# Attention core of a hybrid decoder trunk: head pairs in 64-row score tiles and 64-column value tiles, mask and row maximum in one vector operation

**Chip, cores, metric.** One Trainium2 chip, all eight cores, each with one batch element of 4096 rows. The metric is device time of the slowest core in microseconds (us).

## The reference, cut to what matters

```python
# per layer: x += 1/2 FFN ; x += mixer ; x += 1/2 FFN   (each between two RMS norms)
# layer 0: RG-LRU mixer, layer 1: sliding-window attention, 16 query heads, 2 key/value heads, head size 64
kk = jnp.concatenate([k_prev, k], axis=2)            # 128 previous + 128 current keys
scores = jnp.einsum('bnqkgd,bnskd->bnkgqs', q, kk) * scale
diff = qi + ATTN_BLOCK - kj
band = (diff >= 0) & (diff < WINDOW)                 # 128 keys, the current one included
scores = jnp.where(valid, scores, NEG_INF)
probs = softmax(concatenate([scores, sink], -1))[..., :-1]
out = jnp.einsum('bnkgqs,bnskd->bnqkgd', probs, vv)
```

## The kernel before

The program is a list of operations in eight tiles of 512 rows. Two tiles are under way at a time ("chains"). A list scheduler in Python, with a duration for every operation, settles the fixed order of each engine and which of the eight PSUM banks an operation gets. A chain may hold six banks. The scheduler asks for one bank at a time:

```python
for h in o.ps:                       # the PSUM banks that operation o uses
    if h.bank is None:
        if not self.free or self.held.get(h.chain, 0) >= self.limit:
            return None
        x = min(f[0] for f in self.free) + (PE_HOP if o.eng == "pe" else HOP)
        if x > r:
            r = x
```

At the start of an attention stage the query buffer `QZ` is cleared, since each of the two heads of a pair gets a full 128-row operand whose other half is zero:

```python
dve(s, lambda e: e.memset(QZ[64:128, :, 0, :], 0.0), [], rQZ, n=4096)
dve(s, lambda e: e.memset(QZ[0:64, :, 1, :], 0.0), [], rQZ, n=4096)
```

The stage then has 16 steps of four heads. Step i, shortened:

```python
hh2 = [Ps(s), Ps(s)]                                     # two PSUM banks
for hp in range(2):
    items = []
    for hf in range(2):                                  # score, then mask added by a matmul with IDENT
        items += group(hh2[hp], [QZ[:, c, hf, n*128:(n+1)*128], IDENT[:, :]],
                       [KT[:, n*128:n*128+256], mk[:, :]], lo=hf*256, hi=hf*256+256)
    mm(s, [hh2[hp]], items, ...)                         # one TensorE group for each bank
for hp in range(2):
    dve(... tensor_reduce(out=max, in_=PS[h.bank], op=max))           # row maximum
    dve(... tensor_scalar(out=neg, in0=max, scalar1=-SCALE, scalar2=NSMAX, op0=mult, op1=min))
    # two exponentials of 128x256 on ScalarE, read from PSUM, with their sums; the sinks' exponential
# phaseB: divide (VectorE); phaseB2: 8 transposes on TensorE, copied out by ScalarE
# phaseC: value product, 8 matmuls of 128 columns with zero-padded values, copied out by ScalarE
```

Phases B, B2 and C run one, two and four steps later. TensorE matmuls of the other chain's FFN are meant to fill the time in which ScalarE and VectorE do the softmax.

## Time and profile before

| | before |
|---|---|
| fast runs | 4862.4, 4862.7 us |
| all runs, median | 4899.4 us |
| profiled run | 4863.6 us, fast, granted clock 0.991 to 0.993 |
| TensorE busy | 4663.1 us of 4863.6 |

In the slow state one die has a lower granted clock (0.83 in such a run here). (The median of 4936 us in the prediction is one of the four runs; the median of the four is 4899.)

### The profile page before, as it was taken

How to read it: one execution, taken by the hardware profiler on the slowest of the kernel's cores; microseconds unless marked ns; L12 is line 12 of the kernel's file. 1: busy time of each engine (PE TensorE's matmuls, PEld its weight loads, DVE VectorE, ACT ScalarE, POOL GpSimd, SP SyncE). 2: the span in 40 equal slices, each digit the busy share in tenths (PEclk: the TensorE clock that was granted, in tenths of full speed). 3: DMA queues.
4: the chain of work that ended last, by engine and by line, in shares of the span. 5: the costliest groups of instructions: out<-in, count | busy, mean ns of one | idle time of the engine just before them, and what ended most of it. 6: DMA issues, size and time to landing. Idle time of an engine off the chain costs nothing.

```text
span 4863.6 us, 76832 instructions; the slowest of 8 cores (4837.4 to 4863.6 us)
## 1 busy us (share of the span) xinstructions
PE 4663.1 (96%) x24640; PEld 2246.3 (46%) x24640; DVE 2007.6 (41%) x3580; ACT 2239.4 (46%) x4396; POOL 813.7 (17%) x1365
## 2 busy tenths in 40 slices
PE   6999999898999999999999999999999999999998
PEld 3444445453444444445444444454544444445453
DVE  2355326462235442546223553264622455236441
ACT  2556327372246732647225573273721656227451
POOL 2231321311212021121110201012111012011011
PEclk9999999999999999999999999999999999999999
DMA  9999998979988867483875655536456455543445
GB/s 195 186 191 180 203 179 185 191 167 218 208 202 200 186 194 179 125 202 121 240 190 169 174 158 173 161 104 208 140 179 182 161 166 162 161 158 120 142 150 137
DMA packets 238423, 844.59 MB, mean 174 GB/s; under 512 B 26448, under 2 KB 26704, under 8 KB 238032
## 3 DMA queue, kind: packets, MB, share of 16 engines
q1 hardware_dynamic: 171648, 615.77, 38.4%
q0 software_dynamic: 66384, 223.90, 29.1%
q8 instruction: 209, 3.42, 0.3%
q14 instruction: 182, 1.49, 0.1%
HBM read 932.89 MB, written 113.77 MB: 215 GB/s over the span
## 4 chain that ended last, share of the span: by engine, by line
PE 80%; DMA 7%; ACT 4%; issue 4%; DVE 3%; POOL 2%; SPq 0%; DVEq 0%; POOLq 0%; ACTq 0%
PE psall L333 78%; DMA W<-wgu 2%; DMA W<-wdn 2%; PE psall L427 2%; ACT XN L800 1%; DVE XT L415 1%; DMA X<-x 1%; DMA W<-wmix 1%; POOL NS L406 1%; DMA bdn<-W 1%; PE psall L840 1%; DMA W<-bgu 0%; DMA out<-X 0%; POOL NS L404 0%; DMA W<-bdn 0%
## 5 line engine op out<-in xcount | busy, mean ns | idle before, releaser
L333 PE MATMUL psall<-XN,W 128*128 128x512 bf16 x12864 | 2840.4, 380 | 23.5 <-DMA W<-wgu 13.8
L333 PEld LDWEIGHTS psall<-XN,W 128*128 128x128 bf16 x12864 | 1252.7, 98 | 1513.6 <-issue 56.4
L333 PE MATMUL psall<-W,BIG 128*128 128x512 bf16 x5632 | 1242.4, 380 | 27.2 <-DMA W<-wdn 20.7
L547 DVE TENSOR_TENSOR BIG<-SG,psall 128x512 bf16<-128x512 bf16 x704 | 477.1, 685 | 1149.0 <-PE psall L333 1059.8
L545 ACT ACTIVATE SG<-psall 128x512 bf16<-128x512 f32 x704 | 414.4, 595 | 1108.5 <-PE psall L333 1080.4
L333 PEld LDWEIGHTS psall<-W,BIG 128*128 128x128 bf16 x5632 | 549.1, 98 | 688.1 <-issue 45.9
L568 ACT ACTIVATE HY<-psall 128x512 bf16<-128x512 f32 x256 | 150.5, 595 | 808.8 <-PE psall L333 808.8
L573 DVE TENSOR_TENSOR FB<-psall,GR 128x512 f32<-128x512 f32 x240 | 157.5, 686 | 788.6 <-ACT HY L568 410.8
L404 POOL TENSOR_SCALAR NS<-NS 128x1 f32<-128x1 f32 x256 | 133.1, 520 | 1118.4 <-ACT BIG L515 806.9
L432 ACT ACTIVATE XN<-psall 128x1024 bf16<-128x1024 bf16 x192 | 196.3, 1022 | 264.5 <-PE psall L427 263.4
L406 POOL TENSOR_TENSOR NS<-NS,NHALF 128x1 f32<-128x1 f32 x384 | 305.5, 798 | 51.6 <-POOL NS L404 9.0
L415 DVE SCALAR_TENSOR_TENSOR XT<-X,NS,GI 128x1024 bf16<-128x1024 f32 x192 | 244.9, 1279 | 141.1 <-POOL NS L406 127.9
L800 ACT ACTIVATE XN<-psall,ST 128x256 bf16<-128x256 f32 x512 | 246.5, 509 | 1.5 <-DVE ST L820 0.9
L333 PE MATMUL psall<-W,HY 128*128 128x512 bf16 x1024 | 234.5, 379 | 10.9 <-ACT FB L846 3.9
L411 ACT ACTIVATE XT<-X 128x1024 bf16<-128x1024 f32 x192 | 202.3, 1056 | 54.7 <-DVE X L467 26.4
L972 POOL DMA_DIRECT2D W<-wgu x199 | 110.2, 555 | 693.1 <-PE psall L333 565.2
L791 DVE TENSOR_REDUCE ST<-psall 128x1 f32<-128x512 f32 x256 | 168.7, 683 | 137.2 <-PE psall L333 137.1
L467 DVE SCALAR_TENSOR_TENSOR X<-FB,NS,X 128x1024 f32<-128x1024 f32 x160 | 205.1, 1282 | 40.8 <-POOL NS L406 38.7
L972 POOL DMA_DIRECT2D W<-wdn x143 | 77.2, 540 | 739.4 <-PE psall L333 679.2
L427 PE MATMUL psall<-IDENT,XT 128*128 128x128 bf16 x1536 | 119.5, 224 | 80.0 <-DVE XT L415 67.6
L427 PEld LDWEIGHTS psall<-IDENT,XT 128*128 128x128 bf16 x1536 | 99.4, 100 | 135.6 <-issue 111.5
L333 PEld LDWEIGHTS psall<-W,HY 128*128 128x128 bf16 x1024 | 97.6, 98 | 129.4 <-issue 17.6
(95 smaller groups left out, 3166.3 us busy)
## 6 DMA issues: line engine op xcount, KB each, us to landing
W<-bgu SPq DMA_DIRECT2D x505, 512.0 KB, 4.0
W<-bdn SPq DMA_DIRECT2D x209, 512.0 KB, 3.7
W<-wgu POOLq DMA_DIRECT2D x199, 512.0 KB, 13.6
W<-wdn POOLq DMA_DIRECT2D x143, 512.0 KB, 12.5
W<-bmix SPq DMA_DIRECT2D x117, 512.0 KB, 4.1
bgu<-W SPq DMA_DIRECT2D x88, 512.0 KB, 9.5
W<-wmix POOLq DMA_DIRECT2D x51, 512.0 KB, 10.5
GI<-rows SPq DMA_DIRECT2D x48, 512.0 KB, 5.7
```

The lines of the kernel that those rows point to most:

```text
L333: ins = e.matmul(out() if callable(out) else out, lhsT=lhs() if callable(lhs) else lhs, rhs=rhs() if callable(rhs) else rhs, start=st, sto ...
L406: pool(s, lambda e: e.tensor_tensor(out=NS[s][:, o:o + 1], in0=NS[s][:, i:i + 1], in1=NHALF[:, :], op=ALU.pow), [("NS", s, i), "NHALF"], [ ...
L411: act(s, lambda e: e.activation(out=XT[s][:, b % 2, :], in_=X[s][:, b, :], func=AF.Square, scale=1.0 / 32, accum_out=NS[s][:, 16 + b:17 + b]),
L415: dve(s, lambda e: e.scalar_tensor_tensor(out=XT[s][:, b % 2, :], in0=X[s][:, b, :], scalar=NS[s][:, 20 + b:21 + b], in1=GI[s][:, :], op0= ...
L427: ins = e.transpose(PS[h.bank].bitcast(BF16)[:, c * 128:(c + 1) * 128], XT[s][:, b % 2, c * 128:(c + 1) * 128], IDENT[:, :])
L432: act(s, lambda e: e.activation(out=XN[s][:, :, b * 128:(b + 1) * 128], in_=PS[h.bank].bitcast(BF16).rearrange("p (c q) -> p c q", c=NCH), ...
L467: dve(s, lambda e: e.scalar_tensor_tensor(out=X[s][:, b, :].rearrange("p (h t) -> p h t", h=2), in0=FB[s][:, c:c + d + 1:d, :], scalar=R, ...
L545: act(s, lambda e, g=g, hg=hg: e.activation(out=SG[s][:, g, :], in_=PS[hg.bank], func=AF.Silu), [hg], [("SG", s, g)], tab="silu", ps=[hg])
L547: dve(s, lambda e, g=g, j=j, hu=hu: e.tensor_tensor(out=A[:, j, :], in0=SG[s][:, g, :], in1=PS[hu.bank], op=ALU.mult), [("SG", s, g), hu], ...
L791: dve(s, lambda e, h=h, mxc=mxc: e.tensor_reduce(out=ST[s][:, kk, mxc:mxc + 1], in_=PS[h.bank], axis=AX.X, op=ALU.max), [h], [("ST", s, kk ...
L800: act(s, lambda e, h=h, hf=hf, hh=hh, ngc=ngc: e.activation(out=EEs[kk][:, hh, :], in_=PS[h.bank][:, hf * 256:(hf + 1) * 256], func=AF.Exp ...
L972: return e.dma_start(out=W[:, slot, 0:ncols], in_=ap[:, 0:ncols])
```

## The change

The intent: do the two heads of a pair at once in the upper and the lower 64 rows of the array, without zero padding; do the value product in two column halves at once; add the mask where the row maximum is taken, on VectorE. The core of the diff (layout, value copies with their two small memsets of 128x256, and checks at the end are cut):

```diff
+            need = sum(h.bank is None for h in o.ps)
+            if need:
+                if len(self.free) < need or self.held.get(o.chain, 0) + need > self.limit:
+                    return None
+                x = sorted(f[0] for f in self.free)[need - 1] + (PE_HOP if o.eng == "pe" else HOP)
...
-            dve(s, lambda e: e.memset(QZ[64:128, :, 0, :], 0.0), [], rQZ, n=4096)
-            dve(s, lambda e: e.memset(QZ[0:64, :, 1, :], 0.0), [], rQZ, n=4096)
...
+                for ci in range(2):
+                    for hf in range(2):
+                        items.append((bank(hh2[hf], ci * 256, ci * 256 + 256),
+                                      Q[hf * 64:hf * 64 + 64, 2 * g + ci, n * 128:(n + 1) * 128],
+                                      KT[hf * 64:hf * 64 + 64, n * 128:n * 128 + 256], True, True))
+                mm(s, hh2, items, rQ[2 * g] + rQ[2 * g + 1] + rKT, hh2, n=256)
+                G.ops[-1].occ = 2 * (256 / 2400.0 + 0.02)
...
+                    dve(s, lambda e, ...: e.tensor_tensor_reduce(
+                        out=SP[k2][:, hf, :, :], in0=PS[h.bank]..., in1=mk[:, :]..., scale=-SCALE,
+                        scalar=NSMAX[:, 0:1], op0=ALU.add, op1=ALU.min, accum_out=ST[s][:, kk, ngc:ngc + 1]), ...)
...                      # exponentials now read SP in SBUF
+                for k2 in range(2):
+                    for hf in range(2):
+                        items.append((lambda hf=hf: PS[h.bank][hf * 64:hf * 64 + 64, 0:256],
+                                      VP[:, n + k2, hf * 64:hf * 64 + 64], PT4[:, hf, k2, :, :], k2 == 0, k2 == 1))
```

Since a pair of tiles writes two banks, the two score groups of a step have become one TensorE group, and the scheduler now gives it both banks together or none.

More of the change, by code (lines that the diff above doesn't have):

```diff
@@ L158, in ready @@
         if self.banks:
-            for h in o.ps:
-                if h.bank is None:
-                    if not self.free or self.held.get(h.chain, 0) >= self.limit:
-                        return None
-                    x = min(f[0] for f in self.free) + (PE_HOP if o.eng == "pe" else HOP)
-                    if x > r:
-                        r = x
+            need = sum(h.bank is None for h in o.ps)
[3 more added lines that the diff above has]
+                x = sorted(f[0] for f in self.free)[need - 1] + (PE_HOP if o.eng == "pe" else HOP)
+                if x > r:
+                    r = x
         return r
@@ L287, in build_program @@
         KC = sb("KC", [128, 128], BF16)
-        VC = sb("VC", [128, 2, 128], BF16)
+        VC = sb("VC", [128, 128], BF16)
         NHALF = sb("NHALF", [128, 1], F32)
@@ L367, in build_program @@
         dve(P, lambda e: e.memset(KC[:, :], 0.0), [], ["KC"], n=128)
-        dve(P, lambda e: e.memset(VC[:, :, :], 0.0), [], ["VC"], n=256)
+        dve(P, lambda e: e.memset(VC[:, :], 0.0), [], ["VC"], n=128)
         dve(P, lambda e: e.tensor_scalar(out=NSINK[:, :], in0=BC[:, 128:144], scalar1=-1.0, scalar2=None,
@@ L708, in attn @@
             BIGb = BIG[s][:, :].bitcast(BF16)
-            QZ = BIGb[:, 0:8192].rearrange("p (c h t) -> p c h t", c=8, h=2)
-            KT = BIGb[:, 8192:8192 + 128 + T]
-            VP = BIGb[:, 8832:8832 + (NB_ + 1) * 256].rearrange("p (b h m) -> p b h m", b=NB_ + 1, h=2)
-            rQ = [bigu(s, c * 512, (c + 1) * 512) for c in range(8)]
-            rQZ = bigu(s, 0, 4096)
-            rKT = bigu(s, 4096, 4416)
-            rVP = bigu(s, 4416, 4416 + (NB_ + 1) * 128)
+            Q = BIGb[:, 0:4096].rearrange("p (c t) -> p c t", c=8)
+            KT = BIGb[:, 4096:4096 + 128 + T]
+            VP = BIGb[:, 4736:4736 + (NB_ + 1) * 128].rearrange("p (b m) -> p b m", b=NB_ + 1)
+            SP = [BIG[s][:, 2816 + kk * 1024:2816 + (kk + 1) * 1024].rearrange("p (f c q) -> p f c q", f=2, c=2)
+                  for kk in range(2)]
+            rQ = [bigu(s, c * 256, (c + 1) * 256) for c in range(8)]
+            rKT = bigu(s, 2048, 2368)
+            rVP = bigu(s, 2368, 2368 + (NB_ + 1) * 64)
+            rSP = [bigu(s, 2816 + kk * 1024, 2816 + (kk + 1) * 1024) for kk in range(2)]
             XNf = XN[s][:, :, :].rearrange("p c t -> p (c t)")
@@ L728, in attn @@
                 early_io(s, final)
-            dve(s, lambda e: e.memset(QZ[64:128, :, 0, :], 0.0), [], rQZ, n=4096)
-            dve(s, lambda e: e.memset(QZ[0:64, :, 1, :], 0.0), [], rQZ, n=4096)
-            dve(s, lambda e: e.memset(VP[:, 1:NB_ + 1, 0, 64:128], 0.0), [], rVP, n=256)
-            dve(s, lambda e: e.memset(VP[:, 1:NB_ + 1, 1, 0:64], 0.0), [], rVP, n=256)
             dve(s, lambda e: e.tensor_copy(out=KT[:, 0:128], in_=KC[:, :]), ["KC"], rKT, n=128)
-            dve(s, lambda e: e.tensor_copy(out=VP[:, 0, :, :], in_=VC[:, :, :]), ["VC"], rVP, n=256)
+            dve(s, lambda e: e.tensor_copy(out=VP[:, 0, :], in_=VC[:, :]), ["VC"], rVP, n=128)
             pc = Piece(("akv",))
@@ L750, in attn @@
             dve(s, lambda e: e.tensor_tensor(
-                out=VP[:, 1:NB_ + 1, 0, 0:64], in0=psv()[:, :, 0:64],
-                in1=BC[:, 0:64].unsqueeze(1).broadcast_to([128, NB_, 64]), op=ALU.add),
-                [hv, "BC"], rVP, n=256, ps=[hv])
-            dve(s, lambda e: e.tensor_tensor(
-                out=VP[:, 1:NB_ + 1, 1, 64:128], in0=psv()[:, :, 64:128],
-                in1=BC[:, 64:128].unsqueeze(1).broadcast_to([128, NB_, 64]), op=ALU.add),
-                [hv, "BC"], rVP, n=256, ps=[hv])
+                out=VP[:, 1:NB_ + 1, :], in0=psv(), in1=BC[:, 0:128].unsqueeze(1).broadcast_to([128, NB_, 128]),
+                op=ALU.add), [hv, "BC"], rVP, ps=[hv])
             dve(s, lambda e: e.tensor_copy(out=KC[:, :], in_=KT[:, T:T + 128]), rKT, ["KC"], n=128)
-            dve(s, lambda e: e.tensor_copy(out=VC[:, :, :], in_=VP[:, NB_, :, :]), rVP, ["VC"], n=256)
+            dve(s, lambda e: e.tensor_copy(out=VC[:, :], in_=VP[:, NB_, :]), rVP, ["VC"], n=128)
             for pq in range(4):
@@ L765, in attn @@
                     proj(s, pc, c2 * 1024, XN, "XN", h)
-                    for hf in range(2):
-                        act(s, lambda e, c=c, hf=hf, h=h: e.activation(
-                            out=QZ[hf * 64:hf * 64 + 64, c, hf, :], in_=PS[h.bank][hf * 64:hf * 64 + 64, :],
-                            func=AF.Identity, bias=PV[hf * 64:hf * 64 + 64, BQ + c:BQ + c + 1], scale=1.0),
-                            [h, "PV"], rQ[c], ptr=1, ps=[h])
+                    act(s, lambda e, c=c, h=h: e.activation(
+                        out=Q[:, c, :], in_=PS[h.bank], func=AF.Identity, bias=PV[:, BQ + c:BQ + c + 1], scale=1.0),
+                        [h, "PV"], rQ[c], ptr=1, ps=[h])
             steps = [(n, g) for n in range(NB_) for g in range(4)]
@@ L778, in phaseA @@
                 mk = MASK0 if (k == 0 and n == 0) else MASK
+                k2 = i % 2
                 hh2 = [Ps(s), Ps(s)]
-                for hp in range(2):
-                    c = 2 * g + hp
-                    items = []
+                items = []
+                for ci in range(2):
                     for hf in range(2):
-                        items += group(hh2[hp], [QZ[:, c, hf, n * 128:(n + 1) * 128], IDENT[:, :]],
-                                       [KT[:, n * 128:n * 128 + 256], mk[:, :]], lo=hf * 256, hi=hf * 256 + 256)
-                    mm(s, [hh2[hp]], items, rQ[c] + rKT + ["IDENT", "MASK", "MASK0"], [hh2[hp]], n=256)
@@ L787, in phaseA @@
-                for hp in range(2):
-                    h = hh2[hp]
-                    mxc = 0 if hp == 0 else 14
-                    ngc = 1 if hp == 0 else 15
-                    dve(s, lambda e, h=h, mxc=mxc: e.tensor_reduce(
-                        out=ST[s][:, kk, mxc:mxc + 1], in_=PS[h.bank], axis=AX.X, op=ALU.max),
-                        [h], [("ST", s, kk, 0, hp)], ps=[h])
-                    dve(s, lambda e, mxc=mxc, ngc=ngc: e.tensor_scalar(
-                        out=ST[s][:, kk, ngc:ngc + 1], in0=ST[s][:, kk, mxc:mxc + 1], scalar1=-SCALE,
-                        scalar2=NSMAX[:, 0:1], op0=ALU.mult, op1=ALU.min),
-                        [("ST", s, kk, 0, hp), "NSMAX"], [("ST", s, kk, 1, hp)], n=4, ptr=1)
-                    for hf in range(2):
-                        hh = 2 * hp + hf
-                        act(s, lambda e, h=h, hf=hf, hh=hh, ngc=ngc: e.activation(
-                            out=EEs[kk][:, hh, :], in_=PS[h.bank][:, hf * 256:(hf + 1) * 256],
-                            func=AF.Exp, bias=ST[s][:, kk, ngc:ngc + 1], scale=SCALE,
+                        items.append((bank(hh2[hf], ci * 256, ci * 256 + 256),
+                                      Q[hf * 64:hf * 64 + 64, 2 * g + ci, n * 128:(n + 1) * 128],
+                                      KT[hf * 64:hf * 64 + 64, n * 128:n * 128 + 256], True, True))
@@ new lines, in phaseA @@
+                mm(s, hh2, items, rQ[2 * g] + rQ[2 * g + 1] + rKT, hh2, n=256)
+                G.ops[-1].occ = 2 * (256 / 2400.0 + 0.02)
+                G.ops[-1].dur = G.ops[-1].occ + 0.17
+                for hf in range(2):
+                    h = hh2[hf]
+                    ngc = hf
+                    dve(s, lambda e, h=h, hf=hf, ngc=ngc: e.tensor_tensor_reduce(
+                        out=SP[k2][:, hf, :, :], in0=PS[h.bank].rearrange("p (c q) -> p c q", c=2),
+                        in1=mk[:, :].unsqueeze(1).broadcast_to([128, 2, 256]), scale=-SCALE, scalar=NSMAX[:, 0:1],
+                        op0=ALU.add, op1=ALU.min, accum_out=ST[s][:, kk, ngc:ngc + 1]),
+                        [h, "NSMAX", "MASK", "MASK0"], [("ST", s, kk, 1, hf), ("SP", s, k2, hf)]
+                        + (rSP[k2] if hf == 0 else []), ptr=1, ps=[h])
+                    for ci in range(2):
+                        hh = 2 * ci + hf
+                        act(s, lambda e, hf=hf, ci=ci, hh=hh, ngc=ngc: e.activation(
+                            out=EEs[kk][:, hh, :], in_=SP[k2][:, hf, ci, :],
+                            func=AF.Exp, bias=ST[s][:, kk, ngc:ngc + 1], scale=-1.0,
@@ L803, in phaseA @@
                             accum_out=ST[s][:, kk, 2 + hh:3 + hh]),
-                            [h, ("ST", s, kk, 1, hp)],
+                            [("ST", s, kk, 1, hf), ("SP", s, k2, hf)] + rSP[k2],
                             [("EE", s, kk, hh), ("ST", s, kk, 2, hh)] + ([rEE[kk]] if hh == 0 else [])
                             + (rXN if i == 0 and hh == 0 else []),
-                            n=256, ptr=1, tab="exp", ps=[h], acc=True)
-                    act(s, lambda e, hp=hp, ngc=ngc: e.activation(
-                        out=ST[s][:, kk, 6 + 2 * hp:8 + 2 * hp],
-                        in_=BC[:, 128 + 4 * g + 2 * hp:128 + 4 * g + 2 * hp + 2],
+                            n=256, ptr=1, tab="exp", ps_in=False, acc=True)
@@ L811, in phaseA @@
+                    act(s, lambda e, hf=hf, ngc=ngc: e.activation(
+                        out=ST[s][:, kk, 6:10].rearrange("p (c f) -> p f c", f=2)[:, hf, :],
+                        in_=BC[:, 128 + 4 * g:132 + 4 * g].rearrange("p (c f) -> p f c", f=2)[:, hf, :],
                         func=AF.Exp, bias=ST[s][:, kk, ngc:ngc + 1], scale=1.0),
-                        [("ST", s, kk, 1, hp), "BC"], [("ST", s, kk, 3, hp)], n=4, ps_in=False, ptr=1, tab="exp")
+                        [("ST", s, kk, 1, hf), "BC"], [("ST", s, kk, 3, hf)], n=4, ps_in=False, ptr=1, tab="exp")
@@ L853, in phaseC @@
                 items = []
-                for ci in range(2):
-                    items += group(h, [VP[:, n + k2, hf, :] for hf in range(2) for k2 in range(2)],
-                                   [PTs[kk][:, (ci * 2 + hf) * 2 + k2, :] for hf in range(2) for k2 in range(2)],
-                                   lo=ci * 128, hi=ci * 128 + 128)
-                mm(s, [h], items, rVP + rPT[kk] + rXN, [h], n=128)
+                PT4 = PTs[kk].rearrange("p (c f k) q -> p f k c q", c=2, f=2)
+                for k2 in range(2):
+                    for hf in range(2):
+                        items.append((lambda hf=hf: PS[h.bank][hf * 64:hf * 64 + 64, 0:256],
+                                      VP[:, n + k2, hf * 64:hf * 64 + 64], PT4[:, hf, k2, :, :], k2 == 0, k2 == 1))
+                mm(s, [h], items, rVP + rPT[kk] + rXN, [h], n=256)
+                G.ops[-1].occ = 2 * (256 / 2400.0 + 0.05)
+                G.ops[-1].dur = G.ops[-1].occ + 0.17
                 act(s, lambda e: e.activation(
@@ L896, in build_program @@
         emit(nc, G, eng, esem, wsem, vsem, bsem, W, (wgu, wdn, wmix), (bgu, bdn, bmix), limit, report)
+        for sem in bsem:
+            if sem.v:
+                nc.sync.wait_ge(sem.h, sem.v)
         for s in range(NS_):
@@ L901, in build_program @@
                         nc.sync.wait_ge(sem.h, sem.v)
+    mybir.codegen_inst_isa_subclasses(nc)
     return nc
```

## The prediction

> **What bounds the kernel now.** I read the page's engine table first, then the cores, the slices, the groups of instructions, the stretches of the attention core, and last the timeline there.
>
> ```profile
> PE 4663.1 (96%) x24640; PEld 2246.3 (46%) x24640; DVE 2007.6 (41%) x3580; ACT 2239.4 (46%) x4396; POOL 813.7 (17%) x1365
> PEclk9999999999999999999999999999999999999999
> DMA  9999998979988867483875655536456455543445
> PE 80%; DMA 7%; ACT 4%; issue 4%; DVE 3%; POOL 2%; SPq 0%; DVEq 0%; POOLq 0%; ACTq 0%
> ```
>
> TensorE is 96% busy over 4863.6 us, and 80% of the chain that ended last is TensorE; the other engines are below half. Since its ends are modelled, I checked with spacings. A run of 32 matmuls of 512 columns takes 7.07 us, which is 31 spacings and a last one of 0.38, so one spacing is 0.216 us. All 19776 matmuls of that width then fill 4270 us. The 1024 of 256 columns (0.110 us each, below) fill 113, and the 2560 transposes and 1280 other matmuls of 128 columns (0.056) fill 215. That is 4598 of 4864 us, and only some 265 us are gaps. So TensorE time removed should shorten the run almost one for one, unless something else then ends last. All cores are within 0.5% at a clock of 0.99, so this is the fast state; the listed median of 4936 is 1.5% above its fastest run, and I start from 4863.
>
> The attention core appears eight times (one per tile of 512 rows, 16 steps each, 128 steps in all):
>
> ```profile
> 4641.95 0.27 PE L333 MATMUL psall<-BIG 128*128 128x256 bf16 x1
> 4642.06 0.27 PE L333 MATMUL psall<-MASK,IDENT 128*128 128x256 bf16 x1
> ...
> 4642.72 0.27 PE L333 MATMUL psall<-MASK,IDENT 128*128 128x256 bf16 x1
> ...
> 4642.83 0.61 PE L840 MATMUL psall<-IDENT,XN 128*128 128x128 bf16 x8
> ...
> 4645.00 0.61 PE L333 MATMUL psall<-FB,BIG 128*128 128x128 bf16 x8
> ```
>
> The second column is the duration. Eight score and mask matmuls start 0.110 us apart (0.77 us over seven spacings). The eight transposes follow without a gap. The value product is eight matmuls in 0.61 us, of which the last is 0.22, so they are 0.056 us apart. Between these groups stand runs of 8 or 16 matmuls of the other tile's FFN: those are the filler that keeps TensorE busy while ScalarE and VectorE do the softmax.
>
> ```profile
> 790.00:850.00 60.00, 54.32 (x446) 34.05 (x444) 45.98 (x149) 55.45 (x172) 6.40 (x10) 1.00 0.70 170
> ...
> 4435.00:4490.00 55.00, 53.69 (x389) 30.99 (x388) 37.09 (x96) 44.00 (x117) 9.89 (x12) 1.00 0.36 112
> ```
>
> The columns after the length are busy us of PE, PEld, DVE, ACT and POOL, then the clock, the DMA share and GB/s. In the first attention stretch ScalarE is busy 92% of the time and the DMA engines 70%. In the later ones ScalarE is at 80%, TensorE at 98%, DMA at 36%.
>
> [...] The trace shows weight loads of 98 ns hidden behind 256 columns; whether 64-column loads stay hidden no run shows yet. [...] the reduction of 128x512 takes 683 ns, the product with a PSUM operand (L547) 685 ns. So I expect about 0.7 us for the joined operation.
>
> **The change part by part.**
>
> *Score and mask matmuls.* Before: 8 per step by 0.110 = 0.88 us. After: 4 score matmuls in 64-row tiles, alternating upper and lower rows, each pair at once: 2 pairs by 0.110 = 0.22 us. Saved: 0.66 us a step, by 128 = 84 us. Of this the mask alone is 0.44 us a step.
>
> *Value product.* Before: 8 by 0.056 = 0.446 us. After: 4 matmuls of 256 columns, in pairs for the two halves of the columns: 2 by 0.110 = 0.22 us. Saved: 0.226 us, by 128 = 29 us.
>
> *Together* 0.886 us a step, 113 us or 2.3% if tiling were free. [...] Each step goes from full array to row tiles and back, and to column tiles and back: four changes of mode, three where the two groups stand side by side. A full drain would show as the tail that a matmul has beyond its spacing, 0.27 - 0.11 = 0.16 us. Four of them are 0.64 us, which leaves 0.25 us a step (31 us). On the other side, the changed kernel's own schedule table allows 0.02 and 0.05 us above streaming for each pair, 0.14 us a step, which leaves 0.75 (95 us). Those look like fitted numbers, so I lean that way and take 0.25 us of overhead: 0.886 - 0.25 = 0.64 us a step, **81 us** off TensorE.
>
> *VectorE.* 256 reductions (683 ns) become 256 joined operations of about 0.7 us with a 128x512 float32 output; 256 small operations of 207 ns go (51 us busy), and the memsets of L729 to L732 (60 us busy). None of it is on the path, apart from 4.8 us that TensorE spends behind two of the memsets.
>
> *ScalarE.* The query eviction becomes 64 operations of 128x512 in place of 128 of 64x512, which take 682 ns each although they have half the rows: 44 us fewer. The exponentials read float32 from SBUF instead of PSUM. The comparable pair on the page is 689 ns (L656, PSUM) against 714 ns (L670, SBUF), so 512 by 25 ns = 13 us more. ScalarE's work in a step stays about what it is.
>
> *Buffers.* Score banks are freed by VectorE alone, before the exponentials. TensorE now waits 10.0 us for L808 and 8.2 us for L800, mostly for such banks; I credit 5 us. Against it, a step now takes two banks at once.
>
> *Where the saving falls.* Two of the eight attention stretches lie in the first quarter, where weights come in as float32 and DMA is 70% and 50% busy; TensorE waits 34.5 us in all for wgu and wdn. A quarter of 81 us is 20; I take half of that as lost to weights that come no sooner. At the end the last attention core has only the previous tile's last FFN beside it, and needs 16 by 0.64 = 10 us more filler: I take 3 us as lost. Sum: 81 + 5 - 10 - 3 = 73 us. **4863 - 73 = 4790 us**, 1.5% faster.
>
> **The rivals.**
>
> *Mode changes eat it.* If every change drains and the weight load must then follow (another 0.06 us or so, as between a late load and its matmul at the start of such a group), four changes cost 0.9 us, the whole saving, and the time stays at about 4860. [...] Against it: the kernel's own occupancy figures. I give it one in five.
>
> *ScalarE becomes the pace.* In the first attention stretch the evictions of the value product come 3.34 us apart, ScalarE being 92% busy:
>
> ```profile
> 799.78 0.43 ACT L859 ACTIVATE HY<-psall 128x256 bf16<-128x256 f32 x1
> 803.12 0.47 ACT L859 ACTIVATE HY<-psall 128x256 bf16<-128x256 f32 x1
> 806.46 0.51 ACT L859 ACTIVATE HY<-psall 128x256 bf16<-128x256 f32 x1
> ```
>
> Then a step takes what it took, and the TensorE time freed is idle unless more FFN work is put in. For it: that pace. Against it: a tile has four FFNs of 528 matmuls, 114 us each, and the core needs only 10 us more filler, so the freed time comes back as an FFN that ends sooner; and the later stretches have ScalarE at 80%. If it holds for half the stretches, the gain is some 35 us: 4830.
>
> *Free tiling and waits that go too.* If pairs cost nothing (113 us) and half the gaps that TensorE has in the attention core go with the mask matmuls, the gain is 120 to 140 us: 4725 to 4745. For it: about 30 us of waits for L808, L800, L846 and L823 stand there. Against it: those come from the softmax, which isn't shorter.
>
> **Range and chances.** The author's overhead with nothing lost gives 4768, mine 4790, ScalarE's pace 4830, full drains 4860, free tiling 4735. A new order of the whole static schedule adds some 15 us either way. So 4735 to 4860 holds it 8 times in 10. Two per cent is 97 us, 4766: that asks for the author's figure with no loss, or better. I give it 0.25, within 2% 0.72, slower 0.03.
>
> **What would show it.** In the changed kernel's profile: no MASK matmul; the second matmul of a pair starting a few ns after the first (right) or 0.11 us after (tiles not at once); a first matmul after a score or value group that follows within 0.05 us (no drain) or 0.16 us and more (drain); the joined VectorE operation at 0.68 to 0.75 us; exponentials some 25 ns longer; TensorE's busy share still 95% or more. It would be wrong if the share fell below 94% with ScalarE over 90% in all eight stretches, if the joined operation took over 1 us, or if waits for weights grew by more than 20 us.

## The result

| | before | after |
|---|---|---|
| fast runs | 4862.4, 4862.7 | 4721.1, 4721.3, 4724.1 |
| median of all | 4899.4 | 4722.7 |
| ratio of fast runs | | 0.9711 (0.9683 to 0.9739) |

Ratios are the mean time of one kernel's fast runs over that of the other's fast runs of the same rounds, so not quite the ratio of the medians. The gain is 141 us, 2.9%, where 73 us was forecast; 4722.7 lies 12 us below the stated range. The direction was right, the gain forecast was half of what came.

The same lines of the page as the prediction shows, of the kernel after:

```profile
PE 4563.4 (97%) x23616; PEld 2115.3 (45%) x23616; DVE 1929.0 (41%) x3540; ACT 2234.1 (47%) x4348; POOL 791.0 (17%) x1358
PEclk9999999999999999999999999999999999999999
DMA  9999999999988767664774654445466454443544
PE 82%; DMA 8%; issue 3%; DVE 2%; ACT 2%; POOL 2%; SPq 0%; POOLq 0%; DVEq 0%; ACTq 0%
```

TensorE still bounds it. But its busy time fell by 100 us and the span by 143, so over 40 us came from time in which TensorE did nothing. (The busy time counts the tail of a matmul, 380 ns recorded for 512 columns that start 216 ns apart, and a halved clock as busy, so the split by starts below finds more.) The groups of instructions that are new, one shape a line (busy us, mean ns of one, then idle time before):

```profile
L785 DVE CUSTOM_DVE_ANT_1 BIG<-psall,MASK,NSMAX 128x512 f32<-128x512 f32 x256 | 182.8, 747 | 206.6 <-PE psall L333 158.0 <-ACT XN L793 48.6
L793 ACT ACTIVATE XN<-BIG,ST 128x256 bf16<-128x256 f32 x512 | 253.4, 497 | 1.6 <-DVE ST L785 1.2
L333 PE MATMUL psall<-BIG 64*128 64x256 bf16 x512 | 47.4, 274 | 0.0
L333 PE MATMUL psall<-FB,BIG 128*64 128x256 bf16 x320 | 32.8, 283 | 1.0
```

The joined operation takes 747 ns (plus an accumulator read of 83 ns), as expected. The exponentials read SBUF at 497 ns; in the kernel before they took 509 from PSUM, so the loss expected there did not come. With everything else as in the changed kernel, they take 490 from PSUM (run in_psum below), so the source alone makes 7 ns here. And the timeline of TensorE in a core (start, duration):

```profile
3144.41 0.39 PE L333 MATMUL psall<-BIG 64*128 64x256 bf16 x4
3144.73 0.62 PE L833 MATMUL psall<-IDENT,XN 128*128 128x128 bf16 x8
3145.28 0.41 PE L333 MATMUL psall<-FB,BIG 128*64 128x256 bf16 x4
3145.62 0.39 PE L333 MATMUL psall<-BIG 64*128 64x256 bf16 x4
```

Four score matmuls take 0.32 us until the next group starts. Eight transposes, which fill 0.45 us, are followed by the value tiles after 0.55. The starts in the trace say why: the second of a pair starts 3 to 4 ns after the first, the second pair 116 ns (row tiles) or 130 ns (column tiles) after that, and wherever the mode changes the next start is 93 to 97 ns later than the streaming asks (311 ns after a 512-column matmul in place of 216, 149 after a transpose in place of 56, 201 and 205 after the last tile in place of about 108). So pairs do run at once, and **a change of mode costs 0.095 us**, 440 times: 42 us. What fills the 95 ns the trace doesn't separate. Within one mode the next weight load starts some 214 ns ahead of its matmul of 512 columns; after a change, unless TensorE also waited there, the first load starts only 1 to 5 ns ahead, so the late load is part of it or comes with it. The loads that the prediction left open take 107 ns for 64 columns, against 94 for a row tile and 98 in the full array; whether the 130 ns come from that no run shows.

**Where the time went.** For each matmul I took the time to the next start, and split it into streaming (215.8, 108.8 or 55.7 ns for 512, 256 or 128 columns in the full array; for tiles the spacings above), a change of mode (95 ns), and the rest. The rest is waiting, or loss to a halved clock (half of the time that lies in a stretch whose granted clock is 0.5; matmuls of 512 columns start 427 ns apart there). Means of cores 5 and 7 of each profiled run, whose records are complete:

| TensorE, us | before | after | difference |
|---|---|---|---|
| streaming, scores, mask and values | 168.4 | 63.9 | -104.5 |
| changes of mode | 0 | 41.8 | +41.8 |
| waits and halved clock inside the eight attention stages | 75.7 | 41.6 | -34.1 |
| the same, in the 40 us ahead of each stage | 35.0 | 15.3 | -19.7 |
| the same, elsewhere | 110.6 | 82.5 | -28.1 |
| all other streaming | 4424.3 | 4424.3 | 0 |

The matmuls themselves brought 63 us net, less than the 81 of the prediction; waits brought 82, where it had reckoned with a small loss. A second profile of the same kernel (after_again) has some 20 us more of them in all, and 3 to 14 us more in each of the three rows, so small differences in this table mean nothing. The experiments ask where the waits went.

### The profile page after: what moved, and what is told of

It is laid out like the page before. It is cut to its first block, busy times and chain, and to the rows that moved or that the text cites. A ratio compares the mean times of both kernels' runs of the same rounds, so it can differ in the third digit from the quotient of the medians.

```text
span 4720.2 us, 73659 instructions; the slowest of 8 cores (4703.9 to 4720.2 us)
## 1 busy us (share of the span) xinstructions
PE 4563.4 (97%) x23616; PEld 2115.3 (45%) x23616; DVE 1929.0 (41%) x3540; ACT 2234.1 (47%) x4348; POOL 791.0 (17%) x1358
## 4 chain that ended last, share of the span: by engine, by line
PE 82%; DMA 8%; issue 3%; DVE 2%; ACT 2%; POOL 2%; SPq 0%; POOLq 0%; DVEq 0%; ACTq 0%
PE psall L333 80%; DMA W<-wgu 2%; PE psall L427 2%; DMA bgu<-W 2%; DMA W<-wmix 1%; DMA W<-wdn 1%; PE psall L833 1%; DMA X<-x 1%; DVE XT L415 1%; POOL NS L406 1%; DMA out<-X 1%; DMA bdn<-W 0%; DVE BIG L785 0%; POOL NS L404 0%; ACT XN L793 0%
## 5 line engine op out<-in xcount | busy, mean ns | idle before, releaser
L785 DVE CUSTOM_DVE_ANT_1 BIG<-psall,MASK,NSMAX 128x512 f32<-128x512 f32 x256 | 182.8, 747 | 206.6 <-PE psall L333 158.0
L793 ACT ACTIVATE XN<-BIG,ST 128x256 bf16<-128x256 f32 x512 | 253.4, 497 | 1.6 <-DVE ST L785 1.2
L681 DVE TENSOR_TENSOR FB<-FB 128x512 f32<-128x512 f32 x64 | 43.1, 688 | 271.8 <-ACT FB L677 271.8
## 6 DMA issues: line engine op xcount, KB each, us to landing
W<-wdn POOLq DMA_DIRECT2D x133, 512.0 KB, 11.2
W<-wmix POOLq DMA_DIRECT2D x60, 512.0 KB, 11.8
```

What stands on the lines that cost most here:

```text
L785: dve(s, lambda e, h=h, hf=hf, ngc=ngc: e.tensor_tensor_reduce(out=SP[k2][:, hf, :, :], in0=PS[h.bank].rearrange("p (c q) -> p c q", c=2), ...
L793: act(s, lambda e, hf=hf, ci=ci, hh=hh, ngc=ngc: e.activation(out=EEs[kk][:, hh, :], in_=SP[k2][:, hf, ci, :], func=AF.Exp, bias=ST[s][:, ...
```

## The experiments

The table gives the ratio to the kernel before (same rounds, fast runs) and the same split of TensorE time, cores 5 and 7; "stage" is waits and halved clock inside the attention stages, "ahead" those in the 40 us ahead.

| kernel | ratio (95%) | streaming | mode | stage | ahead |
|---|---|---|---|---|---|
| before | 1 | 168.4 | 0 | 75.7 | 35.0 |
| after | 0.9711 (0.9683 to 0.9739) | 63.9 | 41.8 | 41.6 | 15.3 |
| before_no_memsets | 0.9931 (0.9899 to 0.9962) | 168.4 | 0 | 69.4 | 11.3 |
| before_joint | 0.9912 (0.987 to 0.9955) | 168.4 | 0 | 34.8 | 35.1 |
| mask_only | 0.9941 (0.9921 to 0.996) | 112.7 | 0 | 111.7 | 33.3 |
| mask_only_no_memsets | 0.9881 (0.9838 to 0.9923) | 112.7 | 0 | 107.0 | 8.2 |
| joint | 0.9743 (0.9719 to 0.9766) | 112.7 | 0 | 43.4 | 14.3 |
| no_pv_tiles_again | 0.9697 (0.9675 to 0.9719) | 86.8 | 21.3 | 39.7 | 11.8 |
| after_again | 0.9721 (0.9693 to 0.9749) | 63.9 | 41.8 | 45.6 | 18.2 |
| in_psum | 0.9712 (0.9693 to 0.9731) | 62.5 | 42.9 | 47.2 | 14.0 |
| after_memsets | 0.9773 (0.975 to 0.9797) | 64.3 | 41.8 | 57.0 | 26.0 |
| two_steps | 0.9678 (0.965 to 0.9706) | 87.2 | 12.2 | 27.9 | 11.2 |

They ran on three chips, where the kernel before had fast runs of 4865 to 4889 us, so only ratios are compared across rows. (no_pv_tiles had one fast run, not_alternating one: no ratio.) Three of them, before_no_memsets, mask_only_no_memsets and joint, give wrong results: the unused halves of the padded queries hold old values there.

### after_memsets: the two large memsets put back

```diff
+            dve(s, lambda e: e.memset(BIGb[64:128, 0:4096], 0.0), [], rQall, n=4096)
+            dve(s, lambda e: e.memset(BIGb[0:64, 0:4096], 0.0), [], rQall, n=4096)
```

> The changed kernel with the two 64x4096 memsets of the query buffer put back at the start of each attention stage (VectorE, 3.47 us each, of no use to the result). Theory: about 26 us of the gain came from these memsets, which held up the norm at the start of four of the eight attention stages (TensorE gaps of 3.1 and 1.5 to 2.0 us each, then a halved clock for 3.4 to 6.8 us): 4745 to 4752 us, with such gaps and halved-clock stretches back at four starts. Rival: those gaps were an accident of the static schedule, and VectorE has room: 4720 to 4726 us.

Measured: 0.9773 against 0.9711 for the changed kernel, 0.62% or 30 us, near the theory's 26. (The two ratios are from different chips; in_psum, on this run's chip, had 0.9712.) What they do is seen in the kernel before, at the start of a stage. VectorE, then TensorE:

```profile
1983.46 3.47 DVE L730 MEMSET BIG<- 64x4096 bf16 x1 [0.80 <-issue]
1986.85 1.15 DVE L415 SCALAR_TENSOR_TENSOR XT<-X,NS,GI 128x1024 bf16<-128x1024 f32 x1
```

```profile
1982.80 2.54 PE L333 MATMUL psall<-XN,W 128*128 128x512 bf16 x11
1988.27 0.61 PE L427 MATMUL psall<-IDENT,XT 128*128 128x128 bf16 x8 [2.93 <-DVE XT L415]
```

The memset stands in front of the norm's operation on VectorE, and the transposes of the normed rows wait 2.93 us for that. The wait is put down to the norm, not to the memset ahead of it. Twelve us around such a start, in the kernel before and in the kernel after (length, then busy us of PE, PEld, DVE, ACT, POOL, then the granted clock):

```profile
1984.00:1996.00 12.00, 7.43 (x41) 3.64 (x39) 8.74 (x11) 5.16 (x8) 3.52 (x3) 0.86 0.41 135
3183.00:3195.00 12.00, 7.43 (x35) 3.36 (x33) 9.18 (x11) 5.42 (x9) 3.75 (x4) 0.72 0.43 145
```

```profile
1936.00:1948.00 12.00, 11.22 (x70) 5.46 (x69) 8.72 (x9) 6.82 (x11) 6.64 (x11) 1.00 1.01 266
3090.00:3102.00 12.00, 11.23 (x71) 5.68 (x70) 8.72 (x9) 6.96 (x11) 5.49 (x9) 1.00 0.73 266
```

TensorE is busy 7.4 us of 12 before and 11.2 after, and before the clock also drops, to 0.86 and 0.72 in the mean of these stretches: its records show stretches of 0.5 that last 3.4, 6.8 or 10.2 us on this core (14.6 us at the end of the span), in which matmuls of 512 columns start 427 ns apart and not 216. Here, with a gap of 2.93 us before one group of transposes and another of 1.64 us after it, the clock is 0.5 from 1990.2 to 1993.6 us. In the kernel before this happens at four of the eight stages: on this core after gaps of 2.93 to 3.08 us, with the clock at 0.5 from 758.0, 1990.2, 3188.3 and 4372.7 us. How long a gap has to be for that, no run shows. With the memsets back in the changed kernel, the halved clock also reaches into the stage (13 us lost there, none without them).

### before_no_memsets: the kernel before without them

```diff
-            dve(s, lambda e: e.memset(QZ[64:128, :, 0, :], 0.0), [], rQZ, n=4096)
-            dve(s, lambda e: e.memset(QZ[0:64, :, 1, :], 0.0), [], rQZ, n=4096)
```

> The kernel before without the two large memsets of the query buffer (wrong result on purpose: the unused half of each padded query holds old values). Putting them back into the changed kernel cost 0.6%. Theory (they delay the norm at the start of four stages whatever the core looks like): ratio 0.992 to 0.995 to the kernel before, the TensorE gaps of 3 us at 755, 1985, 3184 and 4368 us gone. Rival (they only hurt in the schedule that the changed kernel gets): 0.998 to 1.001.

Measured: 0.9931, 33 us; the waits ahead of the stages fell from 35.0 to 11.3 us, those inside by 6. The memsets cost about the same in either kernel (the interval allows 18 to 49 us here); the rival falls.

### mask_only: the joined operation alone

```diff
-                        items += group(hh2[hp], [QZ[...], IDENT[:, :]], [KT[...], mk[:, :]], ...)
+                        items += group(hh2[hp], [QZ[...]], [KT[...]], ...)
-                    dve(... tensor_reduce ...); dve(... tensor_scalar ...)
+                    dve(... tensor_tensor_reduce(out=PS[h.bank], in0=PS[h.bank], in1=mk, ...))
```

> The kernel before with the mask part alone: the joined VectorE operation in place in PSUM, no mask matmuls, scores still full array with zero padding, memsets kept. Theory (TensorE streaming): 512 matmuls by 0.109 us = 56 us less, waits as before: 4803 to 4812 us, joined operation 0.75 us. Rival (the mask matmuls also carried the waits of the core): 20 us more goes, 4780 to 4790 us.

Measured: 0.9941, 29 us. Both expectations failed on the low side. Streaming fell by 55.7 us as reckoned, and 36 of it came back inside the stages, as waits (+13) and halved clock (+23). So the mask matmuls were not simply on the path: without them TensorE stood idle in the same stage. The stages were 81 us long, as before, and little else came in: the matmuls of 512 columns (the FFN's and the projections') that stand inside the eight stages rose from 1640 to 1704, 14 us of work for the 56 us taken out. One stage, core 5, columns as above (ScalarE is busy 73.47 of 80 us):

```profile
3182.00:3262.00 80.00, 71.54 (x528) 40.42 (x526) 58.60 (x182) 73.47 (x219) 8.37 (x10) 0.98 0.24 73
```

### mask_only_no_memsets

The same without the two memsets.

> The mask part alone, and the two large memsets gone as well (wrong result on purpose). The mask part alone gained 29 us where its 56 us of streaming was expected; its core lost 13 us more in waits and 24 us in stretches of halved clock. Theory (the memsets at the start of a stage let the clock drop in a core that is now thinner): both gains come in full and more, ratio 0.979 to 0.983, halved clock inside the core under 5 us. Rival (the thin core starves by itself): the parts add, 0.9941 - 0.0069 = 0.987, with the 24 us of halved clock still there.

Measured: 0.9881, near the rival's 0.987. The halved clock inside the stage stayed (23 us); the memsets aren't its cause. The thin core starves by itself.

### joint: one TensorE group for both banks, still no tiles

```diff
+            need = sum(h.bank is None for h in o.ps)      # the changed kernel's claim, as in the diff above
...
-                for hp in range(2): ... mm(s, [hh2[hp]], items, ...)
+                items = [all four matmuls of both banks]
+                mm(s, hh2, items, rQ[2 * g] + rQ[2 * g + 1] + rKT, hh2, n=256)
```

> As mask_only_no_memsets, and both score banks claimed by one TensorE group, as the changed kernel does (wrong result on purpose). Theory (in mask_only TensorE waits 26 us between the two score groups of a step, which one group can't): 20 to 26 us less than mask_only_no_memsets, waits in the core at 45 to 60 us as in the changed kernel. Rival (the wait only moves to the front of the group): within 5 us of it, and the fewer waits of the changed kernel come from the score tiles themselves.

Measured: 0.9743, 1.4% or 67 us less than mask_only_no_memsets from an edit that changes no instruction, only what is grouped and in which order it stands. That is far more than the theory's 20 to 26; the waits inside the stage fell from 107 to 43 us and a little came elsewhere. The matmuls of 512 columns inside the stages rose from 1728 to 2336, and TensorE is busy 96% of this one (core 5):

```profile
3122.00:3210.00 88.00, 84.85 (x601) 47.69 (x599) 61.81 (x186) 81.41 (x226) 7.88 (x10) 1.00 0.30 96
```

A kernel with **no tile at all** is thus within 0.3% of the changed one. It is no finished version: a right one would have to clear the padding once, ahead of the stages.

### before_joint: the same edit alone, in the kernel before

> The kernel before with one edit only: the two score groups of a step are one TensorE group of the same 16 matmuls, which claims its two PSUM banks together (mask matmuls, memsets, full array all kept; right result). On top of the mask part this edit was worth 1.4%, since with single claims the attention core takes each bank as it comes free and no FFN matmuls of the other tile stand between its groups. Theory (the claim of banks alone lets the FFN in): TensorE waits in the core fall from 74 to about 45 us, attention stages get longer than 82 us, ratio 0.990 to 0.995. Rival (with 56 us of mask matmuls the core fills TensorE well enough): ratio 0.998 to 1.002, waits in the core at 65 us or more.

(The group has 8 matmuls, not 16.) Measured: 0.9912, 43 us (the interval allows 22 to 63); waits inside the stages fell from 75.7 to 34.8 us, the stages grew from 82 to 88 us, ahead of them nothing changed. The timeline shows what changed. The kernel before, core 7, one and a half steps (the bracket holds the idle time and what ended it):

```profile
3227.79 0.27 PE L333 MATMUL psall<-BIG 128*128 128x256 bf16 x1 [0.30 <-ACT XN L800]
...
3228.88 0.27 PE L333 MATMUL psall<-BIG 128*128 128x256 bf16 x1 [0.50 <-ACT XN L800]
...
3230.08 0.61 PE L840 MATMUL psall<-IDENT,XN 128*128 128x128 bf16 x8 [0.61 <-ACT FB L846]
3230.53 0.61 PE L333 MATMUL psall<-FB,BIG 128*128 128x128 bf16 x8
...
3232.37 0.27 PE L333 MATMUL psall<-BIG 128*128 128x256 bf16 x1 [0.50 <-ACT ST L808]
...
3233.47 0.61 PE L840 MATMUL psall<-IDENT,XN 128*128 128x128 bf16 x8 [0.50 <-ACT XN L846]
```

Score groups (each of four matmuls), transposes and values of the one chain follow each other, with 0.3 to 0.6 us of idling at each, waiting for ScalarE to finish with a bank. From 3226.9 to 3239 us no FFN matmul runs. The same place in before_joint, core 5:

```profile
3203.45 0.27 PE L333 MATMUL psall<-BIG 128*128 128x256 bf16 x1
...
3204.32 0.61 PE L839 MATMUL psall<-IDENT,XN 128*128 128x128 bf16 x8
3204.77 0.61 PE L333 MATMUL psall<-FB,BIG 128*128 128x128 bf16 x8
3205.21 1.89 PE L333 MATMUL psall<-XN,W 128*128 128x512 bf16 x8
3206.94 0.27 PE L333 MATMUL psall<-BIG 128*128 128x256 bf16 x1
...
3207.81 1.89 PE L333 MATMUL psall<-XN,W 128*128 128x512 bf16 x8
```

A run of eight FFN matmuls (`psall<-XN,W`, 1.7 us of streaming) stands between the groups, and the idling is gone. So it is in all eight stages (cores 5 and 7): the matmuls of 512 columns inside them rise from 1640 to 2032, and the longest time without one, between 12 and 18 us in a stage of the kernel before, is between 3 and 5. The reading is this. With single claims, the score groups take each bank as ScalarE frees it, so the attention chain goes on alone at ScalarE's pace. When a score group must find two banks free at once, the FFN's groups, which need one, get banks in between. The stretches show it too (before, then before_joint; columns as above):

```profile
2010.00:2092.00 82.00, 76.23 (x589) 46.44 (x588) 59.49 (x182) 75.41 (x220) 6.56 (x9) 1.00 0.24 75
```

```profile
2002.00:2086.00 84.00, 80.97 (x610) 49.13 (x609) 60.75 (x184) 76.73 (x219) 5.62 (x8) 1.00 0.26 83
```

TensorE is busy 93% of the stage before and 96% after that one edit, while ScalarE is near 92% in both: the softmax goes no faster, TensorE has more to do beside it. That this edit does it is shown, in two kernels. That the bank claim is the cause, and not that two groups became one operation for the scheduler, is argued from the order of the groups: no run claims both banks and keeps two groups.

### in_psum: the joined operation writes back into PSUM

```diff
-                        out=SP[k2][:, hf, :, :], in0=PS[h.bank]...
+                        out=PS[h.bank]..., in0=PS[h.bank]...      # exponentials read PSUM again
```

> The changed kernel with the joined operation writing back into its PSUM bank, so the exponentials read PSUM and hold the two banks as long as in the kernel before. Theory (the 28 us fewer waits inside the attention core come from banks freed earlier): 10 to 25 us slower, 4731 to 4746 us, with waits of TensorE for the exponentials back. Rival (banks don't matter, 6 or 8 of them are enough): 4717 to 4725 us.

Measured: 0.9712, the same as the changed kernel, stage waits 47 us against 41.6 and 45.6 in its two profiles. Freeing the banks ahead of the exponentials, for which the prediction credited 5 us, is not what cut the waits (each interval is about 0.2 to 0.3% either way, so a few us may hide there).

### no_pv_tiles and no_pv_tiles_again: value product in the full array

```diff
-                    items.append((..., VP[:, n + k2, hf * 64:hf * 64 + 64], PT4[:, hf, k2, :, :], ...))   # 64-column tiles
+                    items += group(h, [VP[:, n + k2, hf, :] ...], [PTs[kk][...] ...])                     # zero-padded, 128 columns
```

> The changed kernel with the value product back to the full array with zero padding. Theory (each change of tiling mode costs 0.095 us): the 64-column value tiles save 57.1 - 31.2 = 26 us of streaming and pay 216 changes = 20.5 us, net 5 us, so 4724 to 4731 us here. Rival (the prediction's split, half its overhead on this part): net 13 us, 4732 to 4738 us.

> The changed kernel without the value tiles, a second time because the first had one fast run. Its undisturbed cores were at 4698 to 4710 us, against 4704 to 4720 of the changed kernel on another chip. Theory now: the value tiles cost as much as they save (26 us of streaming against 20 us of mode changes, and longer waits), so the ratio to the changed kernel on this chip is 0.997 to 1.001. Rival (first expectation): 1.001 to 1.003.

The first had one fast run, with a lower clock on one die, and decides nothing. The second: 0.9697 against 0.9721 for the changed kernel on the same chip, 12 us faster without the value tiles; the intervals overlap. The split agrees that they don't pay: 22.9 us of streaming saved, 20.5 us of mode changes and some 12 us of waits added (5.9 inside, 6.4 ahead). No gain from them is seen; whether they cost anything isn't clear of noise. (The run also moves the buffer SP, to make room for padded values.)

### after_again

> The changed kernel itself on the same chip as the three others, so that they are compared with it and not with a ratio from another chip: 0.970 to 0.973 of the kernel before, whatever the theory.

0.9721, as on the first chip within 0.1%. Its spans differ from the first profile by up to 25 us on the same core number, and its waits inside the stages by 4 us, so single profiles carry differences of that size.

### not_alternating: the four matmuls ordered tile by tile

```diff
-                for ci in range(2):
-                    for hf in range(2):
+                for hf in range(2):
+                    for ci in range(2):
```

> The changed kernel with the four matmuls of each group ordered tile by tile (upper, upper, lower, lower) in place of alternating. Theory ([...]): three slots in place of two, 0.11 us more for each of 256 groups = 28 us, ratio to the changed kernel 1.006. Rival (the engine finds the pairs itself): no change. Rival (tiles at once are worth nothing, the gain is from elsewhere): no change either, with second starts 0.11 us apart.

One fast run, 4733.2 us against 4730.9 and 4735.1 for the changed kernel on that chip. The times are those of the first rival: from the first start to the third it is 120 ns in both kernels for row tiles and 133 for column tiles, and a whole score group takes the same (0.32 us until the next group starts):

```profile
3144.11 0.39 PE L333 MATMUL psall<-BIG 64*128 64x256 bf16 x4
3144.43 0.62 PE L833 MATMUL psall<-IDENT,XN 128*128 128x128 bf16 x8
```

The trace doesn't name the tile of a record. But if a tile does one matmul at a time and needs for its 256 columns about the 109 ns of the full array, which no run shows apart, the group fits into its 0.32 us (0.095 of them a change of mode) only with both tiles busy from the start, so the third in program order would have begun with the first. The second record fits that: in every group on cores 5 and 7 it starts 6 to 7 ns after the first, two steps of the 3 to 4 ns that it takes in the changed kernel. That is an inference from times, on the estimate of what one tile can do, and from one fast run.

### two_steps: a version that may beat both

The kernel without value tiles, and the scores of two steps in one group of eight matmuls.

```diff
+                for j in (i, i + 1):
+                    pend[j] = hh2 = [Ps(s), Ps(s)]
+                    ...                                   # items of both steps, at even i only
+                mm(s, hs, items, reads + rKT, hs, n=256)  # claims four banks
```

> A version that may beat both: the changed kernel without value tiles, and the score matmuls of two steps in one group of eight, which needs four PSUM banks at once. Theory (each change of mode costs 0.095 us and some 112 of 224 go): 10 us less than no_pv_tiles, ratio to the kernel before 0.967 to 0.969. Rival (four banks at once starve the FFN beside it): 0.970 to 0.980, with TensorE waits for the joined operation or for evictions up by 10 us or more.

Measured: 0.9678, fast runs 4708.5 to 4712.5 us, correct. Mode changes fell from 21.3 to 12.2 us and stage waits from 39.7 to 27.9: the larger claim didn't starve the FFN, it let more of it in. Eight score matmuls take 0.55 us, and 24 FFN matmuls follow:

```profile
3127.55 0.61 PE L333 MATMUL psall<-BIG 64*128 64x256 bf16 x8
3128.10 5.35 PE L333 MATMUL psall<-XN,W 128*128 128x512 bf16 x24
```

Against the changed kernel (0.9711 and 0.9721) that is 0.3 to 0.4% less, from different chips and each against the kernel before; the intervals overlap. It has the lowest ratio of all runs; that it is faster than the changed kernel isn't clear of noise.

## Why the prediction was off

The direction and the bound were right. The sum was half of what came, and the time fell below the range that was given 8 chances in 10; a large part of the gain lay in a step that the prediction had entered as a cost.

- **Streaming saved** (113 us): 104.5 measured, with the extra spacing of the pairs (116 and 130 ns in place of 109) included. Right.
- **Overhead of tiling** (0.25 us a step, 32 us): the changes of mode were 0.095 us each and 42 us in all, where the prediction put a full drain at 0.16 (its author's estimate, from a record of 0.27 us and a spacing of 0.11; that TensorE drains no run shows) and the kernel's own figures came to 18 us in all. With the wider pair spacings, the net is 63 us and not 81. The doubt was well placed; the lean towards the author's figures was wrong.
- **Which part pays.** The prediction gave scores and mask 84 us and values 29 us of streaming. Measured apart: the mask matmuls bring 29 us alone and about 49 us where the joint claim stands (from 0.9912 - 0.0069, the memsets taken as additive, to 0.9743); the row tiles and what goes with them about 22 us (0.9743 to 0.9697, on two chips, with intervals that meet), of which the split finds only 5 us in the matmuls (25.9 of streaming saved, 21.3 of mode changes paid); the value tiles no gain that is seen. The tiles, which are the change's main intent, thus brought the least.
- **Memsets** ("4.8 us that TensorE spends behind two of the memsets", and not even in the sum): 33 us. The failure was of reading: it counted only waits that named the memset. Those were of the two small memsets (L731, L732); the large ones stood in front of the norm on VectorE, under whose name the wait is listed, and at four stages the clock was 0.5 for 3.4 or 6.8 us after it. The 60 us of VectorE time were passed over with "None of it is on the path", VectorE being busy 41% of the span; what matters is which operation stands behind it at that moment.
- **Buffers** ("I credit 5 us. Against it, a step now takes two banks at once"): the step that failed. Taking two banks at once, entered as a cost, gained 43 us alone in the kernel before and 67 us on top of the mask part, more than any other edit from the same starting kernel (memsets 33, mask 29, though these intervals overlap). It changed the order in which the scheduler mixes the two chains. The prediction looked for freed banks (in_psum: worth nothing measurable) and not at who gets them.
- **ScalarE as the pace** (rival, 4830 us): this is what mask_only shows. There TensorE time taken out came back as waits and halved clock, because the schedule put little in its place. The argument against it, that the core only needs 10 us more filler, was sound about the amount of work and silent on whether it could get a bank. The joint claim is what kept this rival from coming true in the changed kernel.
- **Free tiling and waits that go too** (4725 to 4745): nearest to the time, by luck in part: its reason held by half. Tiling wasn't free (42 us of mode changes); the waits went, but the claim there that "those come from the softmax, which isn't shorter" was wrong: the softmax stayed and the waits fell by 34 us. The "about 30 us" of waits that it started from were 76 by the split.
- **Losses at the start and the end** (13 us): not seen; waits outside the stages fell by 28 us beyond those ahead of them, among them those for weights (48.7 us on the profiled core before, 32.0 after). No run isolates that; it moves with the whole static schedule, and stays open.

Along one path of runs from the kernel before to the changed one: joint claim 43, memsets 33, mask 49, tiles and the rest 11 (0.9743 to 0.9721), 136 us. That they come near the 141 proves nothing, since the mask's and the tiles' shares are taken as what is left between two ratios. In another order the shares differ: mask 29 first, then the joint claim 67.

## What to carry to other kernels

When two streams of work share the PSUM banks, look at how each claims them: a stage that takes banks one by one at the pace of a slower engine can shut out the work that should fill its gaps (so the order of the groups suggests here), and removing matmuls from such a stage can mostly make idle time (36 of 56 us here), until the filler can get in. A wait is listed under the last operation ahead of it; ask what stood before that one on its engine before calling its cost small. Tile only where the streaming saved in a group exceeds two changes of mode, here 0.19 us for a group that stands alone, and join groups to pay them less often.
